# Moving the last S5 scan behind the memory norm, the first memory keys and one attention head

## The chip, the cores and the metric

The kernel runs on one core of a Trainium2 chip. The metric is the device time of one execution in microseconds. The engines are PE (matrix products and transposes), DVE (vector operations), ACT (activation functions, copies, and issue of some DMAs), POOL (vector operations and indirect DMAs) and SP (issue of DMAs). PEld is the loading of weights into PE. Each engine works through its own list of instructions in the order in which they stand there, and waits where an operand is not ready.

## The reference

One layer of a hybrid encoder, 512 tokens of width 1024 in fp32, in three residual steps:

```python
proj = rmsnorm(h) @ w_in                       # q, k, v (512 each) and u (512)
att  = chunked_attention(rmsnorm(q), rmsnorm(k), v, rel_bias)   # 8 heads of 64
ssm  = s5_mixer(u, ...)                        # scan, then y = gelu(y); y * sigmoid(y @ w_glu + b)
h    = h + concat(rmsnorm(att), rmsnorm(ssm)) @ w_out
h    = h + memory_attention(rmsnorm(h), rmsnorm(mem), ...)      # 256 memory tokens, 4 heads of 256
h    = h + peer_ffn(rmsnorm(h), ...)           # 16384 experts, 8 heads, top 16
```

The S5 mixer is a complex diagonal recurrence over the 512 tokens, x_t = a x_(t-1) + B u_t, read out as y = Re(C x) + D u, for 32 groups of 16 channels with 64 complex states each. The memory tokens pass through their own norm and the projections w_mk (keys, normalised per head) and w_mv (values).

## The kernel before

`front()` does all up to the PEER part, `peer()` the rest, from about 450 us to the end. Large products run as three fp32r products each (hi by hi, hi by lo, lo by hi, lines 124 to 126): a weight piece is loaded by SP into one of three wraw buffers, ACT copies it to whi (L108) and DVE or POOL makes wlo, the remainder (L110); whi and wlo have four buffers each.

The order in which `front()` issues its work: norm of x; u; the S5 tables; q and k (w_qk), with `scan(0)` to `scan(2)` and `readout(0)`, `readout(1)` among them; v (w_v, line 566); `scan(3)`, `readout(2)`, `readout(3)` and `relay()`; the scaling of q and k by their norms (two products pbc into PSUM and one multiply each, L574 to L576); then what the string `PLAN` says, letter by letter (line 39 and lines 701 to 703); then w_out and the memory attention. The letters of PLAN:

- `m` (`mem_in`): loads mem, normalises it and transposes it (ntp) into M, as Mh (ACT, L185) and Ml (DVE, L186), by `norm_T`.
- `k`, `K` (`mem_k`): memory keys, pv on Mh and Ml with four pieces of w_mk each, kN and sums of squares by ACT; `K` then makes two diagonal tiles dg (DVE, L610), scales and transposes kN by them (pk, L617) and writes mkT (ACT).
- a digit (`att_head`): one attention head: scores pS (L684), bias and row maximum by DVE into asb (L685), exp by ACT (L686), transposes (L689), copy by DVE into apt (L690), the product with v, po (L694), and the scaled result (L698).
- `i` (`glu_in`): Gelu of yT on ACT (L634) and its halves yh (ACT, L636) and yl (DVE, L637). `g` (`glu`): the product pz with w_glu, which needs yh and yl of all four parts.
- `v`, `V` (`mem_v`): memory values.

`scan(q)` makes pb by 8 products (L472), multiplies and adds on DVE (L479 to L484), runs 8 recurrences of 128 steps on DVE (L487) and multiplies back into XX (L491 to L496). `readout(q)` makes py from Ug and XX by 12 products (L504 to L506), which ACT writes over Ug (L507). `relay()` writes Ug to memory (Ys) in 8 DMAs, half of them issued by SP and half by ACT (L515), and reads it back as yT, 1 MB, in one DMA that ACT issues (L518).

This is the order in which work is issued; the order on each engine is then chosen by the list scheduler of the tile framework (line 1216, `schedule_with_timeline_sim=True`), which starts from priorities of issue and puts work of later steps into gaps. What it chose is fixed in the program. Tiles that bind the order: three asb and three apt tiles (shared by scan and heads), two bt tiles, PSUM banks (two for g, two for s, four for a), and `p8`, four large tiles of two halves that XT, M, me, mix and others take in turn; `b8` has ten tiles.

Of the kernel before, what the change touches and what calls it, by code (L numbers as in the profile page):

```python
# [35 lines left out]
    _o += _w  # L36
NVEC = _o
NB8 = 10
PLAN = 'im012kK34g5v6V7'
POG = 0  # L40
LK = "v"
LV = "gv"
# [16 lines left out]
def setup(tc, es):  # L59
    c = Ctx()  # L60
# [24 lines left out]
    def t4(name, dt=F32, w=1024):  # L85
        return c.tp.tile([128, w], dt, tag="t4", name=name, bufs=4)
# [76 lines left out]
        for b, pv in zip(blocks, pvs):  # L163
            evac(b, 0, pv)

    def norm_T(src, blocks, gain, hl, keep=None, gb=None):
        if gb is None:
            gb = t4("gb")
            nc.sync.dma_start(gb, gain.partition_broadcast(128))
        for b in blocks:  # L170
            xn = t4("xn")
            ss = small("nss", [128, 2])
            S.activation(xn, src(b), AF.Square, accum_out=ss[:, 0:1])
            rpow(ss[:, 1:2], ss[:, 0:1], 1.0 / 1024)
            V.scalar_tensor_tensor(xn, src(b), ss[:, 1:2], gb, op0=OP.mult, op1=OP.mult)  # L175
            if keep:
                keep(b, xn)
            for half in range(2):
                pt = pst("s", "ntp")
                for q in range(4):  # L180
                    k = half * 4 + q
                    P.transpose(pt[:, q * 128:(q + 1) * 128], xn[:, k * 128:(k + 1) * 128], c.ident)
                pt3 = pt.rearrange("p (k t) -> p k t", k=4)
                hi, lo = hl[0].part(half, b), hl[1].part(half, b)
                S.activation(hi, pt3, AF.Copy)  # L185
                c.nt_ins = V.tensor_tensor(lo, pt3, hi, op=OP.subtract).ins  # L186
# [29 lines left out]
def front(tc, I, c):  # L216
# [6 lines left out]
    with tc.tile_pool(name="f1", bufs=1) as f1:  # L223
        def b8(shape, name, dt=F32):
            return f1.tile(shape, dt, tag="b8", name=name, bufs=NB8)
# [240 lines left out]
        def scan(q, MT):  # L466
            pb = [pst("s", "pb") for _ in range(2)]
            s_ = slice(q * 4, q * 4 + 4)
            v3 = lambda a: a.rearrange("p (g c) -> p g c", g=4)
            for h in range(2):  # L470
                for z in range(4):
                    P.matmul(pb[h][:, z * 128:(z + 1) * 128], MT[h][:, q % 2 * 4 + z], Ug[:, q * 4 + z], start=True, stop=True)  # L472
            X = t4("XX").rearrange("p (h g c) -> p h g c", h=2, g=4)
            XX.append(X)
            G.memset(X[:, :, :, 0:1], 0.0)
            br, bi = v3(pb[0]), v3(pb[1])
            tr, ti = Tr[:, s_], Ti[:, s_]
            x0, x1, zr_, zi_ = [v3(f(n_)) for n_, f in (("x0", p2), ("x1", p2), ("zr", a2), ("zi", a2))]
            V.tensor_tensor(x0, br, tr, op=OP.mult)  # L479
            V.tensor_tensor(x1, bi, ti, op=OP.mult)  # L480
            V.tensor_tensor(zr_, x0, x1, op=OP.add)
            V.tensor_tensor(x0, bi, tr, op=OP.mult)
            V.tensor_tensor(x1, br, ti, op=OP.mult)
            V.tensor_tensor(zi_, x0, x1, op=OP.subtract)  # L484
            for z in (zr_, zi_):
                for g in range(4):
                    V.tensor_tensor_scan(z[:, g], mag4[:, q * 4 + g:q * 4 + g + 1].broadcast_to([128, 128]), z[:, g], 0.0,  # L487
                                         op0=OP.mult, op1=OP.add)
            n_ = slice(0, 127)
            T = V.tensor_tensor  # L490
            T(x0, zr_, tr, op=OP.mult)  # L491
            T(x1, zi_, ti, op=OP.mult)
            T(X[:, 0, :, 1:128], x0[:, :, n_], x1[:, :, n_], op=OP.subtract)
            T(x0, zr_, ti, op=OP.mult)
            T(x1, zi_, tr, op=OP.mult)
            T(X[:, 1, :, 1:128], x0[:, :, n_], x1[:, :, n_], op=OP.add)  # L496
# [67 lines left out]
            rhl.append((rh, rl))  # L564
        vN = b8([128, 4, 512], "vN")
        gemmN([[I["w_v"][i] for i in range(4)]], XT, range(4), lambda b, ct, p: S.activation(vN[:, b], p, AF.Copy), leng=V)
        scan(3, MT)
        readout(2)
        readout(3)
        relay()  # L570
        for i, (rh, rl) in enumerate(rhl):
            for m in range(4):
                pbc = pst("a", "pbc")
# [8 lines left out]
        def mem_in():  # L582
            M.extend(pair(c.p8, "M", 256))
            me = c.p8([128, 2, 1024], "me", F32)
            nc.scalar.dma_start(me, I["mem"].rearrange("(b p) d -> p b d", p=128))
            norm_T(lambda b: me[:, b], range(2), I["gkv"], M)

        mkv = {}

        def mem_k(ct):  # L590
            if ct == 0:
                mkv["kN"] = b8([128, 2, 1024], "kN")
                mkv["ks"] = small("ks", [128, 2, 4], bufs=1)
            kN, ks = mkv["kN"], mkv["ks"]

            def ev(b, _, p):
                S.activation(kN[:, b, ct * 512:(ct + 1) * 512], p, AF.Copy)
                for e in range(2):
                    S.activation(t2("kj")[:, :256], p[:, e * 256:(e + 1) * 256], AF.Square,
                                 accum_out=ks[:, b, ct * 2 + e:ct * 2 + e + 1])  # L600
            c.gemmK([I["w_mk"][ct * 4 + i] for i in range(4)], M, range(2), ev, leng=LK)
            if ct == 0:
                return
            mkT = mkv["k"] = b8([128, 8, 256], "mkT")
            dg = []
            for b in range(2):
                rk = small("rk", [128, 4])
                rpow(rk, ks[:, b], 1.0 / 256)
                d_ = t2("dg").rearrange("p (h t) -> p h t", h=4)
                V.tensor_tensor(d_, ident.unsqueeze(1).broadcast_to([128, 4, 128]),  # L610
                                rk.unsqueeze(2).broadcast_to([128, 4, 128]), op=OP.mult)
                dg.append(d_)
            for hd in range(4):
                pk = pst("g", "pk")
                for m in range(2):
                    for b in range(2):
                        P.matmul(pk[:, m * 256 + b * 128:m * 256 + (b + 1) * 128], kN[:, b, hd * 256 + m * 128:hd * 256 + (m + 1) * 128],  # L617
                                 dg[b][:, hd], start=True, stop=True)
                for m in range(2):
                    S.activation(mkT[:, hd * 2 + m], pk[:, m * 256:(m + 1) * 256], AF.Copy, scale=vc("gmk", m))  # L620

        def mem_v(ct):
            if ct == 0:
                mkv["v"] = b8([128, 2, 1024], "mv")
            c.gemmK([I["w_mv"][ct * 4 + i] for i in range(4)], M, range(2),
                  lambda b, _, p: S.activation(mkv["v"][:, b, ct * 512:(ct + 1) * 512], p, AF.Copy), leng=LV)
# [71 lines left out]
            V.tensor_tensor(att[:, :, h * 64:(h + 1) * 64], po[:, :256].rearrange("p (b d) -> p b d", b=4),  # L698
                            sm[:, 1].unsqueeze(2).broadcast_to([128, 4, 64]), op=OP.mult)

        todo = {"m": mem_in, "i": glu_in, "g": glu, "k": lambda: mem_k(0), "K": lambda: mem_k(1), "v": lambda: mem_v(0), "V": lambda: mem_v(1)}
        for o in PLAN:
            att_head(int(o)) if o.isdigit() else todo[o]()
        sums = small("sums", [128, 4])
# [515 lines left out]
```

## Time and profile before

| | |
|---|---|
| time, median of 3 runs | 1723.84 us (1723.48 to 1723.87) |
| profiled execution: time, span | 1723.96 us, 1722.2 us |
| mean granted clock of PE | 0.988 |
| PE, DVE, ACT, POOL busy | 97%, 79%, 42%, 39% of the span |
| HBM read, written | 350.30 MB, 34.08 MB |

The stretch that the change touches runs from about 141 us (last products of v and of the last scan's pb) to about 273 us (first product of w_out). All times in the rows are microseconds from the start of the span. A busy time is the union of the records of an engine; records of PE overlap, since products are pipelined, so the step from one start to the next is shorter than a record. One fp32 product leaves two records on PE, one fp32r product or transpose leaves one. Where a row ends in square brackets, the engine was idle for so long before it, and the name behind the arrow is what ended the wait. ACTq and SPq are the issue of DMAs by these engines. In windows, PEclk is the granted clock as a share of 2.4 GHz.

### The profile page before, as it was taken

Reading aid. Unit: us, or ns where it says so; the run is one execution under the profiler, and the core shown is the slowest. Engines: PE = TensorE matmul, PEld = TensorE weight load, DVE = VectorE, ACT = ScalarE, POOL = GpSimd, SP = SyncE. Lnnn points to the kernel's source line nnn. Section 1 sums busy time; section 2 is a strip of 40 time slices with the busy share of each in tenths; the row PEclk is TensorE's granted clock in tenths of the full one; section 3 lists DMA queues with packets and bytes.
Section 4 is the critical chain, followed back from the end, with each engine's and each line's share of the span. In section 5 each row is a group of like instructions: output and inputs, shape, how many; then the busy total and the mean of one; then the engine's idle time right before and its main releaser. Section 6 shows DMA issues by size and latency. Waiting matters only on the chain.

```text
span 1722.2 us, 24846 instructions
## 1 busy us (share of the span) xinstructions
PE 1664.3 (97%) x8929; PEld 1447.9 (84%) x8929; DVE 1351.9 (79%) x2699; ACT 730.3 (42%) x1233; POOL 676.9 (39%) x550
## 2 busy tenths in 40 slices
PE   7997999999999789989999999999999999999999
PEld 6775778877788788879898999999999999998887
DVE  7989664554579989985997977777777777788977
ACT  4343673433343348877443333333333333333332
POOL 5130032441477753200345444444344444344541
PEclk9998999999999889999999999999999999999999
DMA  6422433220522237878549999889889888889996
GB/s 202 112 57 92 137 116 122 91 86 13 184 96 83 94 117 216 241 208 264 177 163 339 338 335 329 304 316 329 291 321 332 311 309 330 324 290 343 349 369 244
DMA packets 158124, 386.34 MB, mean 224 GB/s; under 512 B 14248, under 2 KB 73128, under 8 KB 157872
## 3 DMA queue, kind: packets, MB, share of 16 engines
q1 hardware_dynamic: 107504, 212.83, 36.9%
q0 software_dynamic: 36864, 134.23, 21.7%
q10 hardware_dynamic: 13632, 37.69, 6.3%
q8 instruction: 70, 1.15, 0.3%
q14 instruction: 54, 0.44, 0.1%
HBM read 350.30 MB, written 34.08 MB: 223 GB/s over the span
## 4 chain that ended last, share of the span: by engine, by line
PE 75%; DVE 17%; issue 2%; POOL 2%; DMA 2%; ACT 1%; DVEq 0%; SPq 0%; ACTq 0%; POOLq 0%
PE acc L1098 27%; PE pa L124 9%; PE pa L126 8%; PE pa L125 8%; PE pv L124 3%; PE pv L126 3%; PE pv L125 3%; PE pw L1029 2%; DVE wlo L110 2%; DVE ca L899 1%; PE po L694 1%; DVE ex L920 1%; PE pS L684 1%; DVE xn L175 1%; DMA ug<-in_peer_u_dram,ei 1%
## 5 line engine op out<-in xcount | busy, mean ns | idle before, releaser
L108 ACT ACTIVATE whi<-wraw 128x1024 fp32r<-128x1024 f32 (+1 forms) x332 | 349.6, 1055 | 383.9 <-PE pa L125 230.2
L110 DVE TENSOR_TENSOR wlo<-wraw,whi 128x1024 fp32r<-128x1024 f32 (+1 forms) x278 | 344.9, 1241 | 55.6 <-ACT whi L108 54.6
L124 PE MATMUL pa<-PTh,whi 128*128 128x384 f32 x1024 | 356.4, 348 | 9.1 <-ACT act L1056 9.1
L126 PE MATMUL pa<-PTh,wlo 128*128 128x384 f32 x1024 | 348.1, 340 | 0.0
L125 PE MATMUL pa<-PTl,whi 128*128 128x384 f32 x1024 | 347.2, 339 | 0.0
L973 POOL DMA_INDIRECT vg<-in_peer_v_dram,ei x128 | 186.5, 1457 | 220.3 <-DVE X L974 198.5
L963 POOL DMA_INDIRECT ug<-in_peer_u_dram,ei x128 | 183.1, 1431 | 206.1 <-DVE ug L964 182.4
L1098 PE MATMUL acc<-whi,ah 128*128 128x512 f32 x768 | 238.2, 391 | 0.6 <-ACT ah L1086 0.6
L1098 PE MATMUL acc<-wlo,ah 128*128 128x512 f32 x768 | 237.8, 390 | 1.0 <-DVE wlo L110 1.0
L1098 PE MATMUL acc<-whi,al 128*128 128x512 f32 x768 | 237.2, 390 | 0.0
L124 PEld LDWEIGHTS pa<-PTh,whi 128*128 128x128 f32 x1024 | 195.8, 191 | 13.6 <-ACT act L1056 10.1
L125 PEld LDWEIGHTS pa<-PTl,whi 128*128 128x128 f32 x1024 | 195.7, 191 | 3.5
L126 PEld LDWEIGHTS pa<-PTh,wlo 128*128 128x128 f32 x1024 | 195.0, 190 | 0.0
L1086 ACT ACTIVATE ah<-act 128x384 fp32r<-128x384 f32 x128 | 67.3, 526 | 263.9 <-PE acc L1098 225.3
L974 DVE SCALAR_TENSOR_TENSOR X<-vg,dots,X 128x1024 f32<-128x1024 f32 x128 | 164.4, 1285 | 12.4 <-DMA vg<-in_peer_v_dram,ei 10.9
L110 POOL TENSOR_TENSOR wlo<-wraw,whi 128x1024 fp32r<-128x1024 f32 x54 | 132.0, 2452 | 104.1 <-ACT whi L108 102.0
L964 DVE SCALAR_TENSOR_TENSOR ug<-ug,X 128x1024 f32<-128x1024 f32 x128 | 152.1, 1222 | 25.8 <-DMA ug<-in_peer_u_dram,ei 25.7
L1098 PEld LDWEIGHTS acc<-wlo,ah 128*128 128x128 f32 x768 | 144.0, 188 | 33.0 <-DVE wlo L110 1.7
L1098 PEld LDWEIGHTS acc<-whi,al 128*128 128x128 f32 x768 | 144.1, 188 | 30.9
L1098 PEld LDWEIGHTS acc<-whi,ah 128*128 128x128 f32 x768 | 142.8, 188 | 25.0 <-ACT ah L1086 1.0
L1032 ACT ACTIVATE stg<-pw 128x256 f32<-128x256 f32 x192 | 104.2, 684 | 27.2 <-PE pw L1029 21.7
L1094 DVE TENSOR_TENSOR al<-act,ah 128x384 fp32r<-128x384 f32 x128 | 72.8, 570 | 51.9 <-ACT ah L1086 51.9
(383 smaller groups left out, 2627.6 us busy)
## 6 DMA issues: line engine op xcount, KB each, us to landing
wraw<-in_ut_dram SPq DMA_DIRECT2D x128, 512.0 KB
wraw<-in_peer_v_dram SPq DMA_DIRECT2D x128, 512.0 KB
Wd<-stg SPq DMA_DIRECT2D x24, 1024.0 KB
wt<-Wd ACTq DMA_DIRECT2D x32, 768.0 KB
wraw<-in_w_pq_dram SPq DMA_DIRECT2D x16, 512.0 KB
h<-in_x_dram SPq DMA_DIRECT2D x8, 512.0 KB
wraw<-in_w_qk_dram SPq DMA_DIRECT2D x8, 512.0 KB
wraw<-in_w_mk_dram SPq DMA_DIRECT2D x8, 512.0 KB
```

What stands on the lines that cost most here:

```text
L108: S.activation(hi, raw, AF.Copy)
L110: ins = leng.tensor_tensor(lo, raw, hi, op=OP.subtract).ins
L124: P.matmul(out, lhs[0], rhs[0], start=first, stop=False)
L125: P.matmul(out, lhs[0], rhs[1], start=False, stop=False)
L126: P.matmul(out, lhs[1], rhs[0], start=False, stop=last)
L963: G.indirect_dma_start(out=ug, out_offset=None, in_=I["peer_u"], in_offset=IOX(ap=ei[:, k:k + 1], axis=0))
L964: V.scalar_tensor_tensor(ug, ug, 1.0, c.X0, op0=OP.mult, op1=OP.mult, accum_out=dots[:, k:k + 1])
L973: G.indirect_dma_start(out=vg, out_offset=None, in_=I["peer_v"], in_offset=IOX(ap=ei[:, k:k + 1], axis=0))
L974: V.scalar_tensor_tensor(a0, vg, dots[:, k:k + 1], a0, op0=OP.mult, op1=OP.add)
L1032: S.activation(stg[e][:, :, q * 8 + hf * 4:q * 8 + hf * 4 + 4].rearrange("p i t -> p t i"), pw.rearrange("p (t i) -> p t i", t=4)[:, :, e ...
L1094: c.v_ins = V.tensor_tensor(al, a, ah, op=OP.subtract).ins
L1098: P.matmul(acc[b * 2 + d], l[:, b * 128:(b + 1) * 128], v[r][:, d * 512:(d + 1) * 512], start=n == 0 and l is ah and r == 0, stop=n == 127 ...
```

## The change

The last scan, its readout and the relay become one step `s` of PLAN, behind `mem_in`, `mem_k(0)` and head 0; `i` (Gelu) comes behind heads 1 and 2; K stands behind it as before and head 3 behind K. `readout(2)` stays where it was. The memory norm takes its gain and its scratch from one new tile gx in p8, loads the gain by ACT's queue, and uses the one scratch tile for both blocks of memory tokens; kN moves from b8 to p8.

```diff
-PLAN = 'im012kK34g5v6V7'
+PLAN = 'mk0s12iK34g5v6V7'
...
-    def norm_T(src, blocks, gain, hl, keep=None, gb=None):
+    def norm_T(src, blocks, gain, hl, keep=None, gb=None, xn=None):
         if gb is None:
             gb = t4("gb")
             nc.sync.dma_start(gb, gain.partition_broadcast(128))
+        scratch = xn
         for b in blocks:
-            xn = t4("xn")
+            xn = t4("xn") if scratch is None else scratch
...
-        scan(3, MT)
         readout(2)
-        readout(3)
-        relay()
...
-            norm_T(lambda b: me[:, b], range(2), I["gkv"], M)
+            gx = c.p8([128, 2, 1024], "gx", F32)
+            nc.scalar.dma_start(gx[:, 0], I["gkv"].partition_broadcast(128))
+            norm_T(lambda b: me[:, b], range(2), None, M, gb=gx[:, 0], xn=gx[:, 1])
...
-                mkv["kN"] = b8([128, 2, 1024], "kN")
+                mkv["kN"] = c.p8([128, 2, 1024], "kN", F32)
...
+        def scan_out():
+            scan(3, MT)
+            readout(3)
+            relay()
+
-        todo = {"m": mem_in, ...
+        todo = {"s": scan_out, "m": mem_in, ...
```

Lines of the scan, the readout and the norm move by one in the changed file (L487 becomes L488, L507 L508, L185 L186), those of the pbc products back by two; from the memory keys on they agree.

What the scheduler makes of it shows in the lists of three engines. First PE, in the readout of scan 2 and up to the first memory-key product (pv on Mh; ntp are the transposes of the normed memory, pS on ident those of a head). Before:

```order
L504 MATMUL py<-Ug,Mx 128x128
L505 MATMUL py<-XX,CAr 128x128
L506 MATMUL py<-XX,CAi 128x128
L504 MATMUL py<-Ug,Mx 128x128
L689 MATMUL pS<-ident,asb 128x128 x4
L505 MATMUL py<-XX,CAr 128x128
L182 MATMUL ntp<-ident,xn 128x128 x4
L124 MATMUL pv<-whi,Mh_1502 128x512
```

In the changed kernel, behind the last pbc:

```order
L684 MATMUL pS<-kT,qT 128x512
L684 MATMUL pS<-kT,qT 128x384
L183 MATMUL ntp<-ident,gx 128x128 x4
L684 MATMUL pS<-kT,qT 128x128
L684 MATMUL pS<-kT,qT 128x512
L506 MATMUL py<-XX,CAr 128x128
L689 MATMUL pS<-ident,asb 128x128 x4
L124 MATMUL pv<-whi,Mh_1429 128x512
```

The first transposes of the memory stand among the scores of the first heads now, and the first memory-key product stands ahead of most of the readout of scan 2.

Next DVE, around the last scan (x_1378, x_1379 and zr before; x_1609, x_1610 and zr now). Before, up to its second half:

```order
L480 TENSOR_TENSOR x_1379<-pb,Ti 128x512
L481 TENSOR_TENSOR zr<-x_1378,x_1379 128x512
L482 TENSOR_TENSOR x_1378<-pb,Tr 128x512
L483 TENSOR_TENSOR x_1379<-pb,Ti 128x512
L487 SCALAR_TENSOR_TENSOR zr<-mag_387,zr 128x128 x4
L484 TENSOR_TENSOR zi<-x_1378,x_1379 128x512
L685 ISA asb,asm<-pS,bt 128x512
L685 ISA asm 128x1
L487 SCALAR_TENSOR_TENSOR zi<-mag_387,zi 128x128 x4
L491 TENSOR_TENSOR x_1378<-zr,Tr 128x512
```

In the changed kernel, from the second half to the second dg:

```order
L488 SCALAR_TENSOR_TENSOR zi<-mag_387,zi 128x128 x4
L492 TENSOR_TENSOR x_1609<-zr,Tr 128x512
L493 TENSOR_TENSOR x_1610<-zi,Ti 128x512
L120 TENSOR_SCALAR rv<-ks 128x4
L690 COPY apt<-pS 128x512
L685 ISA asb,asm<-pS,bt 128x384
L685 ISA asm 128x1
L494 TENSOR_TENSOR XX<-x_1609,x_1610 128x4x127
L120 TENSOR_SCALAR rv<-ks 128x4
L110 TENSOR_TENSOR wlo<-wraw,whi 128x512
L610 TENSOR_TENSOR dg<-ident,rk 128x512
L495 TENSOR_TENSOR x_1609<-zr,Ti 128x512
```

The scan, which stood among little else, now stands among the copies of a head, the wlo of w_glu and the dg of the memory keys.

Last ACT, around the relay (Ys and yT). Before:

```order
L507 ACTIVATE Ug<-py 128x512
L686 ACTIVATE asb,asm<-asb,asm 128x256
L185 ACTIVATE Mh_1502<-ntp 128x4x128
L515 DMA Ys<-Ug 16x16x128 x4
L185 ACTIVATE Mh_1502<-ntp 128x4x128
L686 ACTIVATE asb,asm<-asb,asm 128x384
L686 ACTIVATE asb,asm<-asb,asm 128x128
L185 ACTIVATE Mh_1502<-ntp 128x4x128
L518 DMA yT<-Ys 128x4x512
```

In the changed kernel:

```order
L508 ACTIVATE Ug<-py 128x512
L516 DMA Ys<-Ug 16x16x128 x4
L686 ACTIVATE asb,asm<-asb,asm 128x128
L686 ACTIVATE asb,asm<-asb,asm 128x256
L686 ACTIVATE asb,asm<-asb,asm 128x512
L519 DMA yT<-Ys 128x4x512
L686 ACTIVATE asb,asm<-asb,asm 128x384
L686 ACTIVATE asb,asm<-asb,asm 128x128
L686 ACTIVATE asb,asm<-asb,asm 128x512
L634 ACT_TABLE_LOAD
L634 ACTIVATE yT<-yT 128x2048
L686 ACT_TABLE_LOAD
```

The Mh copies are gone from here, and the exps of three heads stand behind the relay's DMA issues and Gelu.

## Rows read from the trace of the kernel before

**Rows 1.** The page: busy shares, and engines' shares of the last chain.
```profile
PE 1664.3 (97%) x8929; PEld 1447.9 (84%) x8929; DVE 1351.9 (79%) x2699; ACT 730.3 (42%) x1233; POOL 676.9 (39%) x550
PE 75%; DVE 17%; issue 2%; POOL 2%; DMA 2%; ACT 1%; DVEq 0%; SPq 0%; ACTq 0%; POOLq 0%
```

**Rows 2.** Windows: length, busy us of each engine, PEclk, DMA share, GB/s.
```profile
141.00:168.40 27.40, 18.44 (x78) 12.04 (x77) 27.12 (x52) 5.74 (x10) 0.72 (x2) 0.75 0.36 128
168.40:224.50 56.10, 56.10 (x332) 44.46 (x332) 34.30 (x86) 35.22 (x86) 3.67 (x8) 1.00 0.41 118
148.00:152.00 4.00, 2.40 (x5) 0.98 (x4) 4.00 (x10) 0.00 (x0) 0.72 (x2) 0.72 0.72 242
156.00:160.00 4.00, 0.00 (x0) 0.00 (x0) 3.83 (x7) 0.00 (x0) 0.00 (x0) 0.50 0.00 0
160.00:164.00 4.00, 3.47 (x19) 3.50 (x20) 4.00 (x11) 0.51 (x1) 0.00 (x0) 0.57 0.02 4
164.00:168.00 4.00, 2.38 (x20) 1.93 (x18) 3.93 (x9) 2.22 (x6) 0.00 (x0) 1.00 0.00 0
```

**Rows 3.** Timeline of PE: start, us, line, operation, out<-in, records, wait before.
```profile
149.98 5.79 PE L684 MATMUL pS<-kT,qT 64*128 64x512 f32 x8 [1.60 <-DVE rv L120]
160.53 0.77 PE L504 MATMUL py<-Ug,Mx 128*128 128x128 f32 x2 [4.76 <-DVE x L482]
...
168.37 0.50 PE L124 MATMUL pv<-whi,Mh 128*128 128x512 f32 x1 [0.69 <-ACT Mh L185]
...
178.44 0.39 PE L125 MATMUL pv<-wlo,Mh 128*128 128x512 f32 x1
178.67 0.40 PE L126 MATMUL pv<-whi,Ml 128*128 128x512 f32 x1
...
224.50 0.48 PE L124 MATMUL pz<-yh,whi 128*128 128x512 f32 x1
```

**Rows 4.** Timeline of DVE, from the last k multiplies to the last scan's end.
```profile
152.35 1.29 DVE L576 TENSOR_TENSOR kT<-kT,pbc 128x512 f32<-128x512 f32 x2
153.55 1.29 DVE L175 SCALAR_TENSOR_TENSOR xn<-me,nss,gb 128x1024 f32<-128x1024 f32 x1
...
158.24 0.69 DVE L480 TENSOR_TENSOR x<-pb,Ti 128x512 f32<-128x512 f32 x1
...
169.24 0.68 DVE L496 TENSOR_TENSOR XX<-x,x 128x508 f32<-128x508 f32 x1
```

**Rows 5.** Groups of DVE, 141 to 236 us: busy, mean ns | idle before, releaser.
```profile
L110 DVE TENSOR_TENSOR wlo<-wraw,whi 128x512 fp32r<-128x512 f32 x4 | 2.8, 696 | 4.5 <-ACT whi L108 4.5
L487 DVE TENSOR_TENSOR_SCAN zi<-mag,zi 128x128 f32<-128x128 f32 x8 | 2.7, 408 | 0.0
```

**Rows 6.** Chain of waits, 185 to 218 us: start, us, what, records.
```profile
187.29 2.18 PE po L694 x20
189.47 1.06 PE pS L684 x4
195.00 1.03 PE po L694 x8
209.97 0.44 PE pS L689 x4
215.09 1.34 PE pk L617 x12
```

**Rows 7.** Timeline of ACT around relay and Gelu.
```profile
172.76 0.60 ACT L507 ACTIVATE Ug<-py 128x512 f32<-128x512 f32 x1 [1.38 <-PE py L506]
...
173.78 3.57 ACTq L515 DMA_DIRECT2D Ys<-Ug  x3
...
180.50 0.39 ACTq L518 DMA_DIRECT2D yT<-Ys  x1
...
186.19 1.91 ACT L634 ACTIVATE yT<-yT 128x2048 f32<-128x2048 f32 x1 [1.65 <-DMA yT<-Ys]
...
193.45 1.28 ACT L686 ACT_TABLE_LOAD   x1
```

More of the change, by code (lines that the diff above doesn't have):

```diff
@@ L699, in att_head @@
                             sm[:, 1].unsqueeze(2).broadcast_to([128, 4, 64]), op=OP.mult)
-        todo = {"m": mem_in, "i": glu_in, "g": glu, "k": lambda: mem_k(0), "K": lambda: mem_k(1), "v": lambda: mem_v(0), "V": lambda: mem_v(1)}
+        def scan_out():
+            scan(3, MT)
+            readout(3)
+            relay()
+        todo = {"s": scan_out, "m": mem_in, "i": glu_in, "g": glu, "k": lambda: mem_k(0), "K": lambda: mem_k(1), "v": lambda: mem_v(0), "V": lambda: mem_v(1)}
         for o in PLAN:
```

## The prediction

> **What bounds the kernel now.** I read the page's shares first [rows 1]: PE is busy for 97% of the span and 75% of the chain that ended last is PE work, with DVE second at 17%. So time can only come from places where PE stands still or runs below full clock, and it is lost wherever a reordering makes PE wait. Next I cut the span into windows around the change [rows 2]. From 141.0 to 168.4 us DVE is busy 27.12 of 27.40 us, while PE has 18.44 us and a granted clock of 0.75. From 168.4 to 224.5 PE is busy all 56.10 us at clock 1.00. So before has one hole, DVE fills it, and behind it PE never waits. The four short windows show its shape: no PE work at all in 156 to 160, and clock 0.50 (1.2 of the 2.4 GHz) there, 0.57 in the next four, 1.00 from 164 on.
>
> PE's own rows [rows 3] name what ends each wait: DVE's rv, then its x, and at last Mh. The four score products from 149.98 on (an fp32 product leaves two records, so x8) take 5.79 us; they hold 1536 columns, and 512 columns (a 384 and a 128) take 1.06 us at full clock [rows 6], so 3.2 us would do. The first memory-key product (pv on Mh) starts at 168.37, after which nothing stops PE. How much is lost? Busy time less what the low clock adds leaves 11.9 us of work: 18.44, less 2.6 for the score products (5.79 − 3.2), less about 3.9 for the overlap of records and for the other rows at half clock. So 27.4 − 11.9 = 15.5 us are lost. The weak term is the 3.9.
>
> DVE's rows [rows 4] say why: after the last k multiplies (152.35) and the memory norm's first block (153.55), the last scan runs from 158.24 to 169.92 (169.24 + 0.68), 11.7 us, about 2 of them other work, and the memory norm's second block waits behind it. PE has only head 0.
>
> **The change, part by part.**
>
> *A, taken out of the hole.* The last scan, readout and relay are issued behind head 0. On DVE the first score row is then reached slightly later: one scan half more of the third scan is ahead of it (1.3 us), one first multiply of the last scan (0.69) is gone, so scores start at about 151.3 instead of 149.98. The norm's first block then ends near 155, its transposes come while PE is still on the slow scores (to 157.8), and the Mh and Ml copies follow. PE has transposes until about 158.9, then memory-key products instead of waiting for 168.37. These first products still run at 1.2 GHz. If the clock returns at 160.1, after at 164.8 stands where before stands at 169.9: 5.1 us; if it returns at 163.5, as before's does [rows 2], 166.4, so 3.5 us. I take the middle, −4.3 (ends −9, all of what PE idles or loses beyond 159, and 0).
>
> *B, the scan among the heads.* Twelve multiplies and adds and eight scan steps are not fewer, they now stand where PE used to be full. From the second half of pb to the second dg (the scaling of the memory keys), DVE issues ten 128x512 operations of the scan at 0.65 (6.5; two multiplies of that size take 1.29 in [rows 4]), eight scan steps (2.7, [rows 5]), and at the same 0.65 each four wlo of 128x512, two score additions, one copy for the heads and two dg (5.85), and two small rows (0.3): 15.35 us, 15.6 with hand-offs. In the same stretch PE has 34 memory-key products at 0.235 (8.0; from 178.44 to 178.67 is one, [rows 3]), seven transposes at 0.11 (0.8), three 128x128 products at 0.22 (0.6), four po (1.03) and 384 score columns (0.8), all by [rows 6]: 11.2 us. PE is late by 15.6 − 11.2 = 4.4, first at the copy that po waits for, then at dg. I take +4.4. The cover that could hide it is other head work, but PE takes its work in the written order. Ends: 0, if DVE reaches its scan before PE ends the pb, and 5.5, if the wlo pieces wait for whi besides (four of them waited 4.5 us together, [rows 5], of which PE felt little).
>
> *C, the relay among the heads.* Before has w_mk products for PE while Ug goes through memory and back. After has, from the last py to the first pz, only heads and eight pk: 40 transposes (4.4), 4608 score columns (9.5), 33 po (8.6 at 0.26) and pk (1.8), by [rows 6] some 24 us, and each step needs an exp from ACT. ACT issues in order. From [rows 7]: evacuation to the fourth Ys issue 4.6 us (172.76 to 177.35), evacuation to yT issue 7.7 (172.76 to 180.50), yT issue to Gelu 5.7 (to 186.19), Gelu 1.91, and then a table load 1.28 before the next exp. So the exps behind the yT issue come 7.8 + 1.0 = 8.8 us after the last py, those behind Gelu 13.4 + 1.9 + 1.3 + 1.1 = 17.7 after. By the written order PE asks for the first after 7.1 us of work (late 1.7) and for the second 6.7 us of work behind that, at 15.6 (late 2.1). The two copies by DVE that follow add 0.65 less overlap each way (0.7 in all). I take +4.5; ends 0 (exps early enough) and 6.5 (17.7 less the 11 us of head work that the earlier exps release).
>
> The row shows that a wait on ACT holds what is behind it: 1.65 us idle before Gelu, with the DMA as releaser, while exps exist [rows 7]. The Trainium skill (Perfetto Trace Analysis, section Tensor Engine Instruction: "ACT/DVE/GPSIMD are strict FIFO") speaks against this change in the same way; if exps could pass Gelu, C would be near 0 and the sum +0.1. The same skill (DMA: Bandwidth & Descriptors, section Bandwidth) has 6.15 us for a 1 MB transfer, where this trace has 5.7 from issue to Gelu; by the page C would be an estimated 0.4 larger. The trace's figure stands.
>
> *The rest.* One head more stands before pz and one less behind it: PE work is the same in sum, and the pz start moves by its 4.5 to 6 us without cost. The memory norm's one scratch tile makes the second block's square wait for the first block's transposes; POOL and DVE have other work there, and 10 to 12 products (2.8 us) lie on PE between the two blocks' transposes. I take 0, and up to 1 if the cover is gone. The gain goes on ACT's DMA queue instead of SP's, behind a load that is early: 0. kN lies in another pool, same size: 0. On SP the h loads now precede all w_out loads; w_out is wanted at 273, so 0, up to +1.5. Everything from w_out on has the same order on each engine: 0. POOL's memset for XX moves with the scan, 0.
>
> **Sum.** −4.3 + 4.4 + 4.5 = +4.6 us. The profiled execution took 1723.96 us, 1.76 around its span of 1722.2, so 1728.56; it lies 0.12 above the median of 1723.84, which gives 1728.4.
>
> **The rivals.**
>
> *1. The stalls stay away.* DVE is at 34.30 of 56.10 us in the stretch where the scan goes [rows 2], so by shares there are 21.8 us of room for 10. If DVE is ahead of PE, and six or more exps are ready when ACT stops, B and C fall to 1 or 2 together, and A stays: 1723.84 − 4.3 = 1719.5, down to 1715 where A is at its end. For it: the shares. Against it: the written order, in which the rows that PE waits for stand behind the scan.
>
> *2. The low clock comes back.* Between the last py and pz PE would do only small heads' products with waits. In [rows 2, 3] the granted clock is 0.50 after waits of 1.6 and 4.76 us. If B's or C's waits bring it to 1.2 GHz for some 8 us of work, this costs 4 to 8 more: 1733 to 1737. It decides from the point where PE's waits in that stretch reach those of the hole (about 4 us at once). Against: the waits I work out are near 2 each. Slower.
>
> *3. The hole only moves.* DVE work to Mh is the same in sum, and A, B and C cancel within 1.5: 1722.5 to 1725.5. The prices are estimates of a few us each with both signs, so this needs only B and C at half. Same.
>
> **How the numbers follow.** Forecast (the stalls come, 1726 to 1731): 50%, of which 41 over 0.2% and 9 within it. Rival 1: 27%, of which 23 faster and 4 within. Rival 2: 6%, slower. Rival 3: 17%, within. What measurement can tell from no change is about 0.2%, 3.4 us. This gives faster 0.23, same 0.30, slower 0.47. For the range, 10% is left out at the low end (A near its end with no stalls, below 1717.5) and some 8% at the high end (rival 2 in full, or all terms at their ends: 0 + 5.5 + 6.5 = +12): 1717.5 to 1734. The likeliest case's own range is 1726 to 1731.
>
> **What the profile after would show.** A: score products from about 151, the first pv on Mh near 159 to 160, and PE busy from there; if pv starts after 165, A is wrong. B: PE idle of 3 to 5 us between the second pb and pk (about 180 to 200), with DVE's apt, XX or dg as releaser; with idle under 1, B is wrong. C: after the last py, idle on PE with ACT's asb or DVE's apt as releaser, and on ACT an idle row before Gelu with the DMA as releaser and PE waiting beside it. In all: the first pz, 224.50 before [rows 3], with one more head ahead of it (some 4.5 us), breaks even at 229; I expect about 233. A pz before 227 is rival 1, a granted clock under 0.9 after 170 is rival 2. The stretch from w_out to the end must have its old length; if not, the forecast is wrong for a reason that is not in it.

## The result and the profile after

The changed kernel takes 1743.45 us (1741.38 to 1746.38, four runs), the kernel before 1723.86: a ratio of 1.0115 with an interval of 1.0103 to 1.0127, so 19.6 us slower. The forecast was 1728.4 us and its range ended at 1734. The direction was forecast, the size was not.

The profiled execution took 1746.38 us with a span of 1744.6 us, the longest of the four. The windows of the changed kernel, in stages of its own (columns as in [rows 2]):

```profile
145.00:165.00 20.00, 16.36 (x44) 9.36 (x43) 18.38 (x35) 5.25 (x13) 0.76 (x2) 0.57 0.44 164
165.00:195.00 30.00, 30.00 (x164) 24.48 (x163) 16.83 (x28) 11.97 (x25) 0.69 (x2) 1.00 0.18 55
195.00:205.00 10.00, 7.36 (x47) 5.66 (x45) 10.00 (x26) 5.25 (x18) 2.41 (x2) 1.00 0.51 179
205.00:218.00 13.00, 11.40 (x76) 8.57 (x74) 6.68 (x23) 4.16 (x14) 0.14 (x1) 1.00 0.55 124
218.00:246.00 28.00, 26.76 (x91) 19.00 (x92) 9.83 (x29) 14.90 (x34) 0.43 (x3) 0.52 0.21 56
246.00:276.00 30.00, 29.07 (x136) 21.75 (x134) 20.43 (x33) 22.74 (x35) 10.61 (x7) 0.99 0.28 97
276.00:285.00 9.00, 9.00 (x41) 7.84 (x41) 5.86 (x7) 2.35 (x4) 6.14 (x3) 0.62 0.81 308
```

The row to see is the fifth: from 218 to 246 us PE is busy nearly throughout, but at a granted clock of 0.52, that is at 1.2 GHz. In [rows 2] the whole stretch from the first memory-key product to the first pz (168.4 to 224.5) ran at 1.00. The share of busy time hides this: PE counts as busy while it does half as much. I call a stretch at 0.50 a low spell. A second, shorter one stands in the last row. The waits in front of these spells show in the timeline of PE (columns as in [rows 3]):

```profile
154.77 3.35 PE L684 MATMUL pS<-kT,qT 64*128 64x512 f32 x4 [1.93 <-DVE kT L574]
...
162.40 0.78 PE L124 MATMUL pv<-whi,Mh 128*128 128x512 f32 x1
...
199.29 1.10 PE L694 MATMUL po<-vN,apt 128*128 128x64 f32 x8 [1.48 <-DVE apt L690]
...
203.45 1.60 PE L617 MATMUL pk<-dg,kN 128*128 128x128 f32 x12 [1.02 <-DVE dg L610]
...
218.73 0.55 PE L689 MATMUL pS<-ident,asb 128*128 128x128 f32 x3 [2.31 <-ACT asb L686]
...
229.80 1.22 PE L684 MATMUL pS<-kT,qT 64*128 64x256 f32 x2 [0.50 <-DVE asm L685]
...
242.12 3.62 PE L617 MATMUL pk<-dg,kN 128*128 128x128 f32 x16
...
248.54 0.48 PE L124 MATMUL pz<-yh,whi 128*128 128x512 f32 x1
...
274.92 1.05 PE L663 MATMUL pss<-ones,sqs 128*128 128x2 f32 x8 [0.94 <-POOL sqs L658]
```

The first pz comes at 248.54, against 224.50 before. The clock falls at about 219.2, half a microsecond after the wait of 2.31 us has ended, and comes back at about 246.5, just behind the sixteen pk records and ahead of pz. In between PE does head work (scores pS, transposes and po), and then pk. ACT, around the relay (as [rows 7]):

```profile
208.77 0.60 ACT L508 ACTIVATE Ug<-py 128x512 f32<-128x512 f32 x1 [1.36 <-PE py L507]
209.39 3.58 ACTq L516 DMA_DIRECT2D Ys<-Ug  x4
213.02 0.40 ACT L686 ACTIVATE asb<-asb,asm 128x128 f32<-128x128 f32 x1 [3.66 <-DVE att L698]
...
217.53 0.39 ACTq L519 DMA_DIRECT2D yT<-Ys  x1
217.97 0.61 ACT L686 ACTIVATE asb<-asb,asm 128x384 f32<-128x384 f32 x1 [3.25 <-DVE apt L690]
...
225.47 1.91 ACT L634 ACTIVATE yT<-yT 128x2048 f32<-128x2048 f32 x1
227.40 1.28 ACT L686 ACT_TABLE_LOAD   x1
```

The exp of 384 columns that PE waits for until 218.73 starts at 217.97, right behind the yT issue. The row names a DVE copy as releaser, but ACT stood at the yT issue, which waits for Ys to land; the first experiment shows it.

**A ledger of PE.** To see where 19.6 us are, I summed over windows of 1 us each PE's idle time, and the busy time times one minus the granted clock, from 45 us to the last transpose of the attention output (paT), behind which all kernels have the same order. What is left of the time of that last paT is PE's work at full clock. It comes out between 287 and 293 us for every kernel of this study (296.5 with 5.5 us of added products), so the two sums account for the differences to within about 3 us. Behind the last paT every profiled execution takes between 1415 and 1420 us more. Each cell below is idle + clock loss in us; the last column is the median time, all others are from the profiled execution:

| kernel | to 130 us | 130 to 175 | 175 to first pz | pz to last paT | last paT | work | time |
|---|---|---|---|---|---|---|---|
| before | 2.6 + 0 | 9.0 + 4.3 | 0 + 0 | 0.3 + 0 | 306.4 | 290.1 | 1723.9 |
| changed | 3.8 + 1.7 | 4.3 + 7.0 | 5.5 + 13.4 | 1.2 + 3.4 | 329.6 | 289.3 | 1743.5 |
| yT on SP | 2.0 + 1.7 | 4.3 + 7.0 | 6.3 + 6.5 | 1.2 + 0 | 319.2 | 290.2 | 1737.0 |
| relay on SP | 2.5 + 0 | 3.6 + 7.2 | 7.4 + 7.8 | 1.2 + 3.4 | 323.5 | 290.3 | 1740.8 |
| Gelu after K, 3 | 1.3 + 0 | 4.1 + 7.4 | 3.5 + 3.4 | 0.5 + 5.1 | 317.1 | 291.9 | 1732.5 |
| no relay wait | 2.5 + 0 | 3.6 + 6.9 | 5.2 + 6.7 | 0.9 + 0 | 316.6 | 290.7 | 1731.6 |
| filler | 1.7 + 0 | 4.1 + 7.3 | 6.2 + 7.9 | 0.4 + 0 | 324.1 | 296.5 | 1742.4 |
| heads without exp | 1.5 + 0 | 4.1 + 7.2 | 4.0 + 0 | 1.2 + 1.7 | 311.2 | 291.4 | 1731.5 |
| dense in relay | 1.4 + 0 | 4.1 + 7.2 | 6.7 + 4.6 | 3.5 + 1.7 | 319.9 | 290.6 | 1735.2 |
| dense block | 1.8 + 0 | 3.6 + 7.3 | 12.7 + 5.0 | 3.5 + 9.3 | 334.8 | 291.6 | 1752.5 |
| wlo on POOL | 2.1 + 0 | 3.6 + 6.8 | 5.0 + 16.9 | 0.3 + 0 | 322.0 | 287.2 | 1738.0 |
| three edits | 2.2 + 0 | 3.6 + 7.2 | 4.3 + 1.8 | 0.4 + 1.6 | 310.7 | 289.6 | 1728.8 |
| s in front, new tiles | 1.4 + 0 | 7.5 + 9.6 | 1.4 + 0 | 0.4 + 0 | 313.1 | 292.7 | 1729.4 |
| scan first | 1.7 + 0 | 7.6 + 9.4 | 2.2 + 1.7 | 0.4 + 0 | 315.1 | 292.1 | 1731.7 |
| s in front, gx only | 1.4 + 0 | 7.6 + 9.6 | 5.0 + 2.1 | 0.4 + 0 | 318.3 | 292.3 | 1737.1 |
| move without gx | 1.9 + 0 | 5.3 + 7.3 | 5.5 + 11.7 | 0.3 + 0 | 322.2 | 290.2 | 1740.9 |

From before to the changed kernel: waits +2.9, clock +21.2, together 24.1; work is 0.8 less, and the two profiled executions lie 22.4 us apart (1746.38 and 1723.96). Of the clock's share 13.4 + 3.4 stand behind the relay, 2.7 in the hole and 1.7 at about 58 us. There PE waited 3.76 us against 1.99, behind eight DMA issues of ACT that took 7.33 us against 5.61. The other runs had 4.75 to 6.24 us for these issues, and all but one no clock loss there (yT on SP lost the same 1.7, behind a wait of 2.02 us), so these 2.9 us (1.2 of waiting, 1.7 of clock) vary from one execution to the next. Without them 21.2 are left, near the 19.6 of the medians.

### The profile page after: what moved, and what is told of

The parts are those of the page before. It is cut to its first block, busy times and chain, and to the rows that moved or that the text cites. A ratio compares the mean times of both kernels' runs of the same rounds, so it can differ in the third digit from the quotient of the medians.

```text
span 1744.6 us, 24848 instructions
## 1 busy us (share of the span) xinstructions
PE 1682.3 (96%) x8929; PEld 1459.5 (84%) x8929; DVE 1352.3 (78%) x2699; ACT 730.1 (42%) x1233; POOL 673.5 (39%) x550
## 3 DMA queue, kind: packets, MB, share of 16 engines
q0 software_dynamic: 36864, 134.23, 21.2%
## 4 chain that ended last, share of the span: by engine, by line
PE 75%; DVE 15%; DMA 3%; POOL 3%; issue 2%; ACT 2%; ACTq 0%; SPq 0%; DVEq 0%; POOLq 0%
PE acc L1103 29%; PE pa L124 8%; PE pa L126 8%; PE pa L125 8%; PE pv L124 2%; PE pv L126 2%; PE pv L125 2%; PE pw L1034 2%; DVE wlo L110 2%; PE pS L684 1%; DVE oB L1029 1%; PE po L694 1%; POOL ev L924 1%; DVE oAE L1025 1%; DVE ca L904 1%
## 5 line engine op out<-in xcount | busy, mean ns | idle before, releaser
L978 POOL DMA_INDIRECT vg<-in_peer_v_dram,ei x128 | 182.3, 1424 | 225.1 <-DVE X L979 204.9
L979 DVE SCALAR_TENSOR_TENSOR X<-vg,dots,X 128x1024 f32<-128x1024 f32 x128 | 164.3, 1284 | 13.4 <-DMA vg<-in_peer_v_dram,ei 12.4
L904 POOL TENSOR_TENSOR cx<-tf 128x8 f32<-128x8 f32 (+6 forms) x120 | 44.0, 399 | 175.4 <-ACT tf L897 175.0
```

Of the source, the lines that this page charges most:

```text
L978: G.indirect_dma_start(out=vg, out_offset=None, in_=I["peer_v"], in_offset=IOX(ap=ei[:, k:k + 1], axis=0))
L979: V.scalar_tensor_tensor(a0, vg, dots[:, k:k + 1], a0, op0=OP.mult, op1=OP.add)
```

## The experiments

**The yT read on SP.** One line of `relay()`; the order of PE, DVE and POOL does not change.

```diff
-            nc.scalar.dma_start(yT[0], Ys.rearrange("(m g) ch j c -> (g ch) m (j c)", m=4))
+            nc.sync.dma_start(yT[0], Ys.rearrange("(m g) ch j c -> (g ch) m (j c)", m=4))
```

> The changed kernel, but the read of yT is issued by SP instead of ACT; PE, DVE and POOL keep their order, ACT only loses this one issue. Theory (the 2.31 us wait of PE at 216.4 us, for an exp that stands behind the yT issue on ACT, lets the granted clock fall to 0.50 from 218.9 to 246.3, which costs 13.7 us): this wait goes, PE runs about 6 us further at full clock, and then waits some 4 us for the exps behind Gelu, at about 222 to 227, and the clock falls there. 1735 to 1741 us, with the fall of the clock moved from 219 to about 225. Rival (head work alone, without any wait, is too light for the full clock): the clock falls at about 219 as before, and the time is 1740 to 1744.

Measured: 1737.01 us (ratio 1.0076, 1.0051 to 1.0100). PE's waits between 205 us and pz, and the windows around them:

```profile
221.15 0.70 PE L684 MATMUL pS<-kT,qT 64*128 64x256 f32 x2 [0.50 <-DVE asm L685]
224.95 1.50 PE L689 MATMUL pS<-ident,asb 128*128 128x128 f32 x5 [3.10 <-ACT asb L686]
```

```profile
205.00:221.00 16.00, 15.62 (x100) 11.45 (x98) 8.16 (x29) 6.19 (x16) 0.29 (x2) 1.00 0.67 181
221.00:225.00 4.00, 0.75 (x3) 0.35 (x3) 0.17 (x3) 3.90 (x5) 0.14 (x1) 0.92 0.01 2
225.00:238.00 13.00, 13.00 (x43) 9.30 (x44) 6.83 (x19) 6.41 (x18) 0.14 (x1) 0.50 0.07 20
238.00:256.00 18.00, 18.00 (x92) 13.23 (x90) 10.65 (x21) 12.97 (x24) 2.62 (x3) 1.00 0.30 103
```

The wait of 2.31 us is gone, the clock stays at 1.00 over the same head work up to 224, and it falls in the next wait, for the exps behind Gelu. So the yT issue held the exp, and the fall of the clock moved with the wait, as the theory had it.

**The whole relay on SP**, Ys too, beside the edit above.

```diff
-                    (nc.sync if j % 2 else nc.scalar).dma_start(
+                    nc.sync.dma_start(
```

> The changed kernel with all eight Ys writes and the yT read issued by SP; ACT issues nothing of the relay; PE's order is the same. Theory (the exps behind the relay's issues on ACT come late): no wait of PE for an exp before Gelu, but yT lands some 3.5 us later and the exps behind Gelu with it, so that one longer wait of 6 to 8 us stays and the clock falls once, as in the run with the yT read on SP: 1737 to 1742 us. Rival (what held the exps was not the issue but DVE's score rows): the first wait of 2.3 us stays and the time is that of the changed kernel, 1742 to 1746 us.

Measured: 1740.82 us (1.0083 to 1.0116). One wait of 4.25 us for an exp, until 224.84, and low clock from 223 to 240: time and place as the theory had them, the wait shorter than its 6 to 8 us.

**No relay wait at all.**

```diff
-            nc.scalar.dma_start(yT[0], Ys.rearrange(...))
+            nc.sync.dma_start(yT[0], I["x"].rearrange("(p m) (h c) -> h p m c", m=4, h=2)[0])
```

> The changed kernel, but yT is filled from the input x by SP instead of from Ys, so that neither the yT read nor Gelu waits for the relay (the S5 result is left out of the output; Ys is still written). Gelu and its halves then come earlier and pz too. Theory (the relay's waits on ACT, and the clock they take down, are the loss): no wait over 1.5 us on PE from 205 us to pz, clock 1.00 from 170 to 260 us, 1720 to 1726 us. Rival (the scan among the heads, or light head work by itself, is the loss): the clock falls between 200 and 240 us all the same, above 1735 us.

Measured: 1731.59 us (1727.9 to 1735.59). Neither expectation holds whole. pz came at 225.4, but PE waited 2.56 us for an exp, and the clock fell from 208.7 to 222.3. On ACT this exp (at 207.89) stands behind Gelu and its two table loads, so Gelu holds the exps behind it even where the relay does not hold Gelu:

```profile
208.54 0.59 PE L689 MATMUL pS<-ident,asb 128*128 128x128 f32 x2 [2.56 <-ACT asb L686]
```

```profile
202.89 1.28 ACT L634 ACT_TABLE_LOAD   x1
204.66 1.91 ACT L634 ACTIVATE yT<-yT 128x2048 f32<-128x2048 f32 x1 [0.49 <-DMA yT<-in_x_dram]
206.59 1.28 ACT L686 ACT_TABLE_LOAD   x1
207.89 0.51 ACT L686 ACTIVATE asb<-asb,asm 128x256 f32<-128x256 f32 x1
```

**Heads without exps.** This tells a wait amid head work from head work by itself.

```diff
-                    c.exp_ins = S.activation(sb[:, o:o + n], ...AF.Exp...)
+                    if h in (1, 2, 3, 4):
+                        V.memset(sm[:, 1, b:b + 1], 1.0)
+                    else:
+                        c.exp_ins = S.activation(sb[:, o:o + n], ...AF.Exp...)
...
+                    src = qT[:, kb % 4, 0:128] if h in (1, 2, 3, 4) else sb[:, kb * 128:(kb + 1) * 128]
-                    P.transpose(pS[...], sb[:, kb * 128:(kb + 1) * 128], ident)
+                    P.transpose(pS[...], src, ident)
```

> The changed kernel, but heads 1 to 4 leave out their exps (the transposes read a part of qT, the sums are set to 1; the output is not the reference's). The order on PE keeps its stretch of 23.7 us of head work and pk between the last py and pz, but nothing there waits for ACT. Theory (waits amid light work take the clock down): clock 1.00 from 205 us to pz, pz near 232 us, 1724 to 1731 us. Rival (light head work alone takes it down): the clock falls to 0.50 between the last py and pz without a wait over 1 us before it, 1735 to 1742 us.

Measured: 1731.52 us (1729.49 to 1737.68). Its windows from the memory keys to the end of pz:

```profile
193.00:206.00 13.00, 10.24 (x77) 8.60 (x76) 11.35 (x37) 2.31 (x10) 2.90 (x3) 1.00 0.37 124
206.00:232.00 26.00, 24.73 (x146) 17.40 (x145) 15.70 (x51) 12.44 (x24) 0.43 (x3) 1.00 0.46 120
232.00:246.00 14.00, 14.00 (x64) 10.35 (x65) 8.10 (x15) 10.09 (x15) 2.55 (x2) 1.00 0.33 116
```

26 us of head work and pk at a clock of 1.00, with no wait over 0.80 us in it; pz at 232. Head work alone does not take the clock down. The kernel before shows the same: its last 14.7 us ahead of pz hold heads and pk without a memory-key product, without a wait and at 1.00:

```profile
209.80:224.50 14.70, 14.70 (x101) 11.61 (x99) 9.09 (x28) 9.88 (x29) 2.09 (x4) 1.00 0.29 94
```

The median is half a microsecond above the range given; the loss that is left is mostly in the hole (4.1 + 7.2).

**Dense filler in heads 2 and 3.**

```diff
+                if h in (2, 3):
+                    for _ in range(8):
+                        P.matmul(po[:, 256:512], M[0](0)[:, 0:128], M[0](0), start=True, stop=True)
                 for kb in range(o // 128):
```

> The changed kernel with added work on PE: in heads 2 and 3, ahead of the transposes of each score group, eight products of Mh by Mh (128x256, fp32r) into the unused half of po, 48 products or some 5.5 us in all at 0.115 us each; nothing reads them. They stand where PE waits for exps, between the last py and pz. Theory (waits amid light head work take the clock down, and dense products would hold it): clock 1.00 from 205 us to pz, and though 5.5 us of work are added, less time than the changed kernel: 1730 to 1738 us. Rival (the clock falls for another reason, or the light work itself is slow): the filler is added on top, 1745 to 1752 us, with the clock at 0.50 after 219.

Measured: 1742.43 us (1.0088 to 1.0122). That is neither the 1730 to 1738 of the theory nor the 1745 to 1752 of the rival. PE did most of the filler ahead of the waits; the wait behind the yT issue is gone, but waits of 2.43 and 2.12 us are left, and the clock fell in the second. The low spell is 10 us (227.5 to 237.7) where the changed kernel has 27. This does not show that dense products end a spell: it began later, the eight filler products inside it ran at 0.50, and the clock came back behind the sixteen pk records, as in the changed kernel:

```profile
231.07 2.05 PE L690 MATMUL po<-Mh 128*128 128x256 f32 x8
...
233.78 3.78 PE L617 MATMUL pk<-dg,kN 128*128 128x128 f32 x16
```

**Dense products between relay and pz.** Dense means here 128x512 products of the memory keys and values, one behind the other. K ahead of the scan, v ahead of glu, in two forms: spread, and as a block.

```diff
-PLAN = 'mk0s12iK34g5v6V7'
+PLAN = 'mk0Ks1i23vg4V567'
...
-PLAN = 'mk0s12iK34g5v6V7'
+PLAN = 'mk0Ksv1i23g4V567'
```

> The changed kernel with PLAN 'mk0Ks1i23vg4V567': scan and relay stay behind the first memory keys and head 0, but K is issued ahead of them and the memory values v ahead of glu, so that some 11 us of dense products (pv) stand between the last py and pz, in pieces, with no more than 4.8 us of head work in a row; in the changed kernel it was 24.5 us of head work and pk. Theory (waits amid light work take the clock down, and it stays down until dense work comes): clock 1.00 after 170 us but for a few us, 1720 to 1730 us. Rival (the waits alone, for exps and the relay, are what costs, whatever stands there): 1734 to 1742 us.

> As the run before, but with PLAN 'mk0Ksv1i23g4V567': the 48 dense products of v stand as one block of 11 us right behind the last py, and then 4 us of head work before pz. Theory: Ys, yT and most of Gelu pass behind the block without a wait of PE; clock 1.00 after 170 us up to pz; 1720 to 1729 us. Rival as there: 1734 to 1742 us.

Measured: 1735.16 us (1.0037 to 1.0081) and 1752.48 us (1.0134 to 1.0186). In the first form the relay passes as hoped, but the waits for DVE have grown, for the scan's x and for K's dg, which now stand beside each other:

```profile
196.86 0.77 PE L505 MATMUL py<-Ug,Mx 128*128 128x128 f32 x2 [2.88 <-DVE x L483]
200.44 2.93 PE L617 MATMUL pk<-dg,kN 128*128 128x128 f32 x12 [2.81 <-DVE dg L610]
```

```profile
195.00:210.00 15.00, 9.70 (x45) 9.14 (x46) 12.28 (x28) 5.73 (x16) 1.86 (x2) 0.54 0.06 18
210.00:234.00 24.00, 23.96 (x128) 18.31 (x128) 9.86 (x25) 11.77 (x21) 0.29 (x2) 1.00 0.71 208
```

From 210 us to pz the clock is at 1.00, but ahead of that it was low for 14 us, where the theory allowed a few, and the time lies in the rival's range (1734 to 1742). The theory's price, 1720 to 1730, left these waits out: from 175 us to pz all waits are 6.7 us and the clock's loss 4.6. So this run does not decide for the theory. The block form has one wait of 5.95 us for an exp at 232.73, and the rest of the heads stand bare at the end of the stage (9.3 us of clock loss behind pz); that forecast failed, and so did the rival's 1734 to 1742.

**Gelu behind K and head 3**, PLAN 'mk0s12K3i4g5v6V7'.

> The changed kernel with PLAN 'mk0s12K3i4g5v6V7': Gelu is issued behind K and head 3, so that the order puts 5.8 us less head work between the relay and pz. Theory (wait behind the yT issue, then low clock until dense products come): the first wait of 2 to 3 us stays, the clock falls at about 219 and comes back some 5 us sooner, so 3 to 6 us less than the changed kernel: 1737 to 1741 us. Rival (only the second wait, behind Gelu and two table loads, matters): no low clock before pz, 1726 to 1730 us.

Measured: 1732.51 us (1.0032 to 1.0067), between the rival's 1726 to 1730 and the theory's 1737 to 1741. The wait behind the yT issue is gone, one of 1.62 us at 225.36 is left, and the clock is low from 227 to 238, and from 196.6 to 203.4 behind the wait of 1.47 us for DVE's copy.

**The wlo of w_glu on POOL.**

```diff
-LG = "v"
+LG = "g"
```

> The changed kernel with LG = 'g': POOL instead of DVE makes the four wlo pieces of w_glu, which takes 2.6 us out of DVE's chain from pb to the second dg. Theory (PE waits there because DVE's chain is longer than PE's work): the waits of 1.48 and 1.02 us at 199 and 203 us shrink to under 1.2 us together; the relay's waits and the low clock behind them stay, so 1740 to 1744 us. Rival (they come from exps, not from DVE): both waits stay as they are.

Measured: 1737.95 us (1.0064 to 1.0116). Both expectations failed: the waits became 1.92 and 1.38 us, and the time is below the 1740 to 1744 of the theory. Of the 2.6 us that DVE was spared, its scan steps took back 1.7, being slower beside POOL (below). The clock now fell behind these waits too (197.8 to 204.7), and again for 27 us from 214.9.

**Three of these edits together**: yT on SP, PLAN 'mk0s12K3i4g5v6V7', LG = "g".

> Three edits together in the changed kernel: yT read by SP, PLAN 'mk0s12K3i4g5v6V7' (Gelu behind K and head 3), wlo of w_glu on POOL. Theory: the waits of PE between 190 us and pz shrink to one or two under 1.5 us, the clock stays at 1.00 from 170 us or is down for under 8 us, 1724 to 1731 us. Rival (each order has its own waits, and taking one away moves it): 1732 us or more.

Measured: 1728.79 us (1.0024 to 1.0049). This is inside the theory's range, though two waits of 1.92 and 1.38 us, for DVE, are left where it had one or two under 1.5. Behind the hole two low spells of under 4 us each are left (199.0 to 202.4 and 222.9 to 226.3) in place of the 27, and 14.7 of the 19.6 us come back with no part of the move undone. It is still slower than before.

**The tiles apart from the move.** The changed kernel with the scan's step in front of PLAN ('sim012kK34g5v6V7', written as the old order); the same without kN's new pool; the move without gx; kN's pool alone in the kernel before; and 'smk0i12K34g5v6V7', the scan in front but memory and head 0 ahead of Gelu.

> The changed kernel with PLAN 'sim012kK34g5v6V7', which is the old order of steps with the new tiles (gx as gain and scratch of the memory norm, gain by ACT's queue, kN in the other pool). Theory (all of the loss comes from the moved scan and relay): 1722 to 1727 us, one hole at 143 to 168 us, no low clock behind it. Rival (the tiles, the single scratch buffer or the early DMA are the cause): above 1735 us.

> The changed kernel with PLAN 'sim012kK34g5v6V7' (old order of steps) and kN back in its old pool: of the change only gx is left (gain by ACT's queue, one scratch tile for both blocks). The run with the old order and both new tiles was 5.35 us over before, the one with kN's pool alone 1.3 us under. If gx is what costs there: 1727 to 1731 us, with the longer waits at 146 to 152 us and the second low clock at 166 to 173 us. If the two edits cost only together: 1721 to 1725 us.

> The changed kernel with its new PLAN, but the memory norm keeps its old tiles (gain by SP, a scratch tile for each block); kN stays in the new pool. If the moved scan and relay make the loss by themselves and gx adds its 5 us: 1735 to 1741 us, with the clock at 0.50 for some 25 us before pz. If the loss needs gx: below 1730 us.

> The kernel before with one edit, kN in the other pool. The run with the old order and the new tiles took 5.35 us more than before. If kN's pool is the cause: 1727 to 1731 us. If gx (gain and scratch of the memory norm) is the cause: 1722 to 1726 us here.

> The changed kernel with PLAN 'smk0i12K34g5v6V7': the scan and relay are back in front, the memory norm, the first keys and head 0 are still issued ahead of Gelu. Theory (the scan's and relay's move is 14 of the 19.6 us, the rest is the tiles): as the run with the old order and the new tiles, 1727 to 1731 us. Rival (issuing the memory norm and the keys ahead of Gelu is what costs): above 1735 us.

Measured: 1729.39 (1.0021 to 1.0044), 1737.05 (1.0054 to 1.0095), 1740.88 (1.0078 to 1.0139), 1722.52 (0.9987 to 1.0006) and 1731.72 us (1.0024 to 1.0051). kN's pool costs nothing by itself. The move without gx costs 16.6 us, with the clock at 0.50 for 24 us ahead of pz, so the loss does not need gx. The two runs with 'sim012…' lie outside both of their expectations, 5.4 and 12.8 us over before. Their price cannot be put on gx, since they are not quite the old order: readout(2) and the scaling of q and k are issued outside PLAN, so a step `s` at its head still comes behind them, where the kernel before has the last scan ahead of both. PE's rows show it, first before, then the run with both tiles:

```profile
143.06 2.05 PE L472 MATMUL pb<-Ug,MT 128*128 128x128 f32 x16
```

```profile
163.14 1.16 PE L473 MATMUL pb<-Ug,MT 128*128 128x128 f32 x8 [0.69 <-ACT Ug L508]
166.62 0.76 PE L505 MATMUL py<-Ug,Mx 128*128 128x128 f32 x2 [2.33 <-DVE x L483]
```

Half of the last scan's pb comes behind the readout of scan 2, PE then waits 2.33 us for that scan, and a second low spell follows at 166 to 173. With the old kN there is besides a wait of 4.85 us for an exp, until 201.99. What gx costs without this shift was not measured. The run with 'smk0i…' has the same hole and lies 0.7 us above its theory's range. The move with all the old tiles was not tried.

**The kernel before with LG = "g".**

> The kernel before with the same edit, LG = 'g'. In it DVE waits 4.5 us for these pieces and PE not at all in that stretch, so nothing is to be gained: 1722 to 1726 us. If POOL's slower operation (2.45 us for 128x1024 against 1.24 on DVE) delays pz: up to 1730 us.

Measured: 1722.66 us (0.9986 to 1.0005): no change, as expected. No version is faster than the kernel before by more than its interval.

## Why the prediction was wrong, step by step

- **What bounds the kernel**: right. Loss is PE's waits and its clock, and nothing behind w_out moved. The 15.5 us put down as lost in the hole are 13.3 in the ledger (9.0 + 4.3).
- **A** (−4.3): the place was right, the size half. Less 3.4 us, by which this execution was late already, the first pv comes at 159.0, as worked out. But the hole's loss went only from 9.0 + 4.3 to 4.3 + 7.0, that is 2.0 us: idle became work at half clock. The scores start at 151.3, less the same 3.4, as forecast; this is luck, since 149.98 + 1.3 − 0.69 is 150.6 and not 151.3.
- **B** (+4.4): right in kind, the copy for po and then dg; 1.48 + 1.02 = 2.5 us.
- **C** (+4.5): half right in kind. The exp behind the yT issue came, 2.31 us for 1.7. The wait for the exps behind Gelu, 2.1, did not: PE at half clock reached them after they were done, and the one wait there, 0.50 us, is put down to DVE's score row. (C's upper end should read 17.7 − 11 = 6.7, not 6.5.)
- Up to here the sum is −2.0 + 2.5 + 2.8 = +3.3, near the +4.6 forecast.
- **The step that failed is the low clock.** The sum has no term for it; it stands only as rival 2, with 6%, "from the point where PE's waits in that stretch reach those of the hole (about 4 us at once)", for "some 8 us of work", 4 to 8 us. The clock fell behind a wait of 2.31 us and stayed low for 27 us, through the head work and pk nearly to pz; 13.4 us, and 3.4 more behind the next wait. By the prediction's own sign, a clock under 0.9 after 170, this is rival 2, at two to four times its price. The threshold was read from the one wait of 4.76 us in [rows 3], although the clock had fallen at about 149.8 already (the 0.72 of 148 to 152 in [rows 2]), 6 us before that wait began, and the waits ahead of its fall were 1.60 us [rows 3] and the 0.47 us below: the rows spoke against the threshold. And the duration was priced without asking what stands behind the wait.

```profile
147.65 0.50 PE L574 MATMUL pbc<-rh,selr 8*128 8x512 f32 x1 [0.47 <-DVE qT L576]
```

- **The rest** was costed at nothing. One head more before pz was free within the 3 us of the ledger's work column. kN's pool was free. The move costs 16.6 us without gx and 19.6 with it, and the times of the two kernels overlap, so little of the loss can be gx.

Shown: the wait behind the yT issue, which goes when SP issues the read, and the clock's fall, which then moves to the next wait; head work without waits at full clock, in two kernels; 14.7 us back in the run with three edits, as the low spells behind the hole shrink from 34 to 7 us. Open: what decides whether the clock falls at a wait. The same wait of 1.47 or 1.48 us for DVE's copy at 196 to 199 us is followed by a fall in two kernels (Gelu after K and 3, filler) and by none in four (changed, yT on SP, relay on SP, no relay wait). The wait of 0.93 or 0.94 us for POOL is followed by a fall in the changed kernel (274.92), with the relay on SP and without exps, and by none with yT on SP. At 58 us a wait of 2.02 us is followed by a fall (yT on SP) and one of 1.99 by none (before). Why a spell ends where it does is open too.

## What to carry to other kernels

Price a new wait on PE not by its length alone but also by the work at half clock that may follow it, and give this a term of its own in the sum: here a wait of 2.31 us cost 13.4 us more behind it. An order in which a long stretch of head work stands together, with its operands coming from an engine that also issues and awaits DMAs, is fragile even where its waits are short. When two orders are compared, add up idle time and busy time times the missing clock; with equal work, these two sums are the difference, here to within about 3 us.

## What the runs showed of the hardware that was not expected

- Waits of 0.89 to 5.95 us amid head work went with a fall of the granted clock to 0.50, in the wait or within 2 us behind it, and it stayed there for 3 to 27 us. The shortest of these waits is in the run with three edits, the longest in the block form. Other waits, of 0.9 to 1.5 us, went with none. In the changed kernel and the runs with yT on SP, the relay on SP, no relay wait and the filler, the long spell ended in the sixteen pk records or within 1 us behind them.
- DVE's recurrence steps were slower beside POOL. Four steps took 1.36 us with POOL idle, as at 191.74 and 196.02 in the changed kernel. In the run with the wlo on POOL, where POOL was at its own subtraction, they took 2.55 and 1.91 us. Its rows on DVE, then on POOL:

```profile
187.66 2.55 DVE L488 TENSOR_TENSOR_SCAN zr<-mag,zr 128x128 f32<-128x128 f32 x4
...
191.32 1.91 DVE L488 TENSOR_TENSOR_SCAN zi<-mag,zi 128x128 f32<-128x128 f32 x4
```

```profile
186.63 2.66 POOL L110 TENSOR_TENSOR wlo<-wraw,whi 128x512 fp32r<-128x512 f32 x2 [14.13 <-ACT whi L108]
190.71 1.29 POOL L110 TENSOR_TENSOR wlo<-wraw,whi 128x512 fp32r<-128x512 f32 x1 [1.42 <-ACT whi L108]
```
